# Gate weights into later tiles of the mixer, a row factor taken sooner, a cast behind the root, and turned tiles of both tokens scaled together

## The chip, the cores and the metric

The kernel runs on one core of one Trainium2 chip. The metric is the device time of one execution in microseconds (us). A core has a matrix engine (TensorE, PE in the profile, with its weight loads as PEld), a vector engine (VectorE, DVE), a scalar engine (ScalarE, ACT), GpSimd (POOL) and a sync engine (SyncE, SP) whose queue (SPq) issues nearly all loads. Each engine works through its own list of instructions in order; semaphores hold an instruction until the work it needs is done.

## The reference

One decoder block in fp32 with a sequence of 256 tokens, model width 2048 and feed-forward width 5632:

```
x = x + 0.5 * swiglu_ffn(rms_norm(x, ffn1_norm), ffn1 weights)
z = rms_norm(x, mix_norm) @ w_in            # 2048 -> 5120: lru_x, lru_gate, sc_b, sc_c, sc_x
xc = causal_depthwise_conv(lru_x, width 4) + bias
h  = rg_lru(xc, w_a, b_a, w_i, b_i, lam)    # gates: block-diagonal, 8 heads of 128x128, then a scan
y_lru = h * gelu(lru_gate)
y_sc  = sc_b * causal_depthwise_conv(sc_c * sc_x, width 3)
x = x + concat(rms_norm(y_lru), rms_norm(y_sc)) @ w_out
x = x + 0.5 * swiglu_ffn(rms_norm(x, ffn2_norm), ffn2 weights)
out = rms_norm(x, final_norm)
rms_norm(x, g) = x * rsqrt(mean(x*x) + 1e-6) * g
swiglu_ffn(x)  = (silu(x @ w_gate) * (x @ w_up)) @ w_down
```

## The kernel before

**Tiles.** The 256 tokens are two tiles of 128 (t = 0, 1). The width of 2048 is four chunks of 512. The residual stays in one tile, `xres`. Weights come from memory in units of 128x4x512 (1 MB): four blocks of 128 input rows by 512 columns.

**Products.** Each fp32 factor is split into a rounded part and a rest: for weights `hi` is a cast on ACT and `lo` is raw minus hi on DVE. Three products stand for one: hi by hi, hi by lo, lo by hi. PE first runs a unit's hi products, then its lo products. So the way of a unit is: SP issues the load into a room of the pool `raws` (three rooms), ACT casts it, DVE takes the rest, PE multiplies. `hi` and `lo` lie in the pool `splits` (two rooms; the feed-forward layers have one more). A room is free again when its last reader is done. Sums are held in eight PSUM banks.

**Feed-forward layers.** The two layers compute sums of products by a scheme that combines blocks, so that fewer products are needed, at the price of more additions on DVE. The start of the first layer is written out by hand in `begin` with the engines' order pinned there: PE begins with the first columns on the unscaled input, while ACT and DVE work out the row factor of the norm (`squares`, then `factor`: sum `tot_n`, `v_n`, root `s_n` on ACT, `y_n`, `q_n`, `r_n` on DVE). The first unit of up weights, `raw_u`, comes in two half loads; its cast `hi_u_start` is in three pieces.

**Norms.** A norm of the mixer or of the second layer (class `Norm`, names `nm` and `n2`) leaves out the row factor 1/sqrt(mean + eps) at first. It needs the residual turned, columns to partitions, and scaled by the gain, split into hi and lo (`xT`). The first three chunks are turned by `cross`: `part` copies the chunk of one token tile into one side of the tile `pair` as two halves of each number, a DMA of SP turns it into a `cross_` tile, and `join` puts the halves together in `pair`. Then ACT writes hi and DVE lo. These are tasks, one step of which is taken between two units (`onward`). The last chunk is turned on PE (`turn`, banks `pt_`). The row factor follows as `factor` and then `rows`: DVE builds two diagonal tiles, PE spreads them over the partitions in bank `pb_`, and DVE copies the bank to `bc`. Results are multiplied by `bc` when they leave PSUM.

**Mixer.** The input projection runs in ten groups of columns (`columns`, loop `order` from L1031), each of four units; unit u of group g has the names in_g_u, with the piece of the projection as g (0 lru_x, 1 lru_gate, 2 to 4 the short convolution; a piece has two halves, so names come twice). A group fills four banks, one per 128 columns. Behind the first group stand `flush`, `nm.factor`, `nm.rows` and the two loads of gate weights (`gate_weights`, L857), 512 KB each, which go through rooms of `raws` (`rawgate_a`, `rawgate_i`) and are split like other weights. Then `lru_x` takes the first group: `half_x` and `zx` (times `bc_nm`), the convolution `xc`, its split `xs`, and the gate products `pgate_a`, `pgate_i`, which stand on PE between the products of later units. The mixer has its own pools; `tmp(tag, name)` takes a tile from them. The tags "d" and "v" are used by the recurrence once its first gates are there, one tile of 128x1024 each.

**Order.** Outside `begin` a scheduler of the kernel language sets the order on each engine from the program and its dependences. Deferred small work (`defer`) is released between units by `pump` and `flush`.

Of the kernel before, what the change touches and what calls it, by code (L numbers as in the profile page):

```python
# [10 lines left out]
F32 = mybir.dt.float32  # L11
F32R = mybir.dt.float32r
U16 = mybir.dt.uint16
AF = mybir.ActivationFunctionType
ALU = mybir.AluOpType
AX = mybir.AxisListType

P = 128
D = 2048
S = 256  # L20
FF = 5632
NT = S // P
KD = D // P
KF = FF // P
CW = 512
NC_D = D // CW
UK = 4
NH = 8
# [21 lines left out]
def hybrid_block(ctx: ExitStack, tc: tile.TileContext, a: dict, out: bass.AP):  # L50
    nc = tc.nc
    Engine.pinned = False
    dve, act, pe = (Engine(tc, e) for e in (nc.vector, nc.scalar, nc.tensor))
# [6 lines left out]
    def defer(cost, fn):  # L60
        pending.append((cost, fn))

    def flush():
        while pending:
            pending.popleft()[1]()

    def pump(budget):

        owed[0] = min(owed[0], 0.0) + budget
        while pending and owed[0] > 0:  # L70
            cost, fn = pending.popleft()
            fn()
            owed[0] -= cost
# [5 lines left out]
    raws = ctx.enter_context(tc.tile_pool(name="raws", bufs=3, side="right"))  # L79
# [3 lines left out]
    def bank(name):  # L83
        return psum.tile([P, 512], F32, tag="ps", name=name)

    def f32(ap):
        return ap.bitcast(F32)
# [62 lines left out]
    def big(name):  # L150

        return bigs.tile([P, UK, 2 * S], F32R, tag="big", name=name)
# [39 lines left out]
    def unit(src, name):  # L192
        return parts_of(load(src, name), name)
# [6 lines left out]
    pair = const.tile([P, NT, CW], F32, name="pair")  # L200
    tasks, moving, sides = deque(), deque(), [0]

    def part(src, turned):

        sides[0] = 1 - sides[0]
        two = pair[:, sides[0]].bitcast(U16)
        act.copy(two.rearrange(flat, b=2), src.bitcast(U16).rearrange(mixed, b=2))
        nc.sync.dma_start(turned.rearrange("p (r c) -> p r c", c=P), two, transpose=True)
        return pair[:, sides[0]]

    def join(two, turned):
        tc.keep_in_program_order(act.copy(two.bitcast(U16).rearrange(mixed, b=2), turned.rearrange(flat, b=2)))
        return quad(two)

    def onward():

        if moving:
            two, _, fn = moving.popleft()
            fn(two)
        if tasks:  # L220
            key, begin, fn = tasks.popleft()
            moving.append((begin(), key, fn))

    def on_the_way():
        return {task[0] for task in tasks} | {entry[1] for entry in moving}
# [18 lines left out]
    class Norm:  # L244
# [28 lines left out]
        def cross(self, c, t, room):  # L273
            x = xres[:, t, c * CW : (c + 1) * CW]
            place = []

            def begin():
                place.append(room(f"cross_{self.name}_{c}_{t}").bitcast(U16))
                return part(x, place[0])

            def store(two):
                v = join(two, place[0])
                if t == 0:
                    self.xT[c] = big(f"xT_{self.name}_{c}")
                for j in range(UK):
                    g = self.gain[:, UK * c + j : UK * c + j + 1]
                    hi, lo = (self.xT[c][:, j, o + t * P : o + (t + 1) * P] for o in (0, S))
                    act.activation(hi, v[:, j], AF.Copy, scale=g)
                    dve.scalar_tensor_tensor(lo, v[:, j], g, f32(hi), op0=ALU.mult, op1=ALU.subtract)

            tasks.append(((self.name, c), begin, store))

# [36 lines left out]

    def columns(w, c0, xT, name):
        ps = [bank(f"ps_{name}_{f}") for f in range(4)]
        for u in range(KD // UK):
            blk = unit(w[u * UK * P : (u + 1) * UK * P, c0 : c0 + CW], f"{name}_{u}")
            assert ("nm", u) not in on_the_way()
            for half in range(2):
                for j in range(UK):
                    x = xT[u][:, j, :]
                    for f in range(4):  # L340
                        wf = blk[j][half][:, f * P : (f + 1) * P]
                        if half == 0:
                            pe.matmul(ps[f], wf, x, start=u == 0 and j == 0, stop=False)
                        else:
                            end = u == KD // UK - 1 and j == UK - 1
                            pe.matmul(ps[f][:, :S], wf, x[:, :S], start=False, stop=end)
            onward()
            pump(1.5)
        return ps

    def product(w, c, us, y, name):
        ps = [bank(f"ps_{name}_{t}") for t in range(NT)]
        cs = slice(c * CW, (c + 1) * CW)
        for i, u in enumerate(us):
            blk = unit(w[u * UK * P : (u + 1) * UK * P, cs], f"{name}_{u}")
            multiply([(ps[t], stationary(y(u), t), i == 0, i == len(us) - 1) for t in range(NT)], blk)
            pump(1.5)
        return ps  # L360
# [36 lines left out]
    def quad(tile):  # L397
        return tile.rearrange("p (j c) -> p j c", j=UK)
# [72 lines left out]
    def ffn(tag, norm, after, opening=False):  # L471
        with (
# [67 lines left out]
            ps = {(m, t): bank(f"ps_{m}{tag}_0_{t}") for m in "gu" for t in range(NT)}  # L540
            ws = {"g": wg, "u": wu}

            def first_columns(m, u, **how):
                return load(ws[m][u * UK * P : (u + 1) * UK * P, :CW], f"{m}{tag}_0_{u}", **how)

            def begin():
# [4 lines left out]
                raw = {("g", 0): first_columns("g", 0, pieces=pieces)}  # L551
# [58 lines left out]
                units.extend(big(f"x{tag}_{u}") for u in range(4))  # L610
                ru, (hi, lo, blk) = raw["u", 0], splits_of("u_start")
                act.copy(hi[:, :2], ru[:, :2])
                act.copy(hi[:, 2:3], ru[:, 2:3])
                norm.squares(3, (dve, act), lambda: pair[:, 0])
                norm.factor()
                act.copy(hi[:, 3:], ru[:, 3:])
                dve.tensor_tensor(lo, ru, f32(hi), op=ALU.subtract)
                n = tokens(1)
                rows = [stationary(norm.xT[0], t) for t in range(NT)]
# [231 lines left out]
    nm = held["nm"]  # L851


    with tc.tile_pool(name="mixer", bufs=1) as mp, tc.tile_pool(name="mixw", bufs=2) as mw:
        wgate = {}

        def gate_weights(key, src):  # L857
            raw = raws.tile([P, NH, P], F32, tag="raw", name=f"rawgate_{key}")
            nc.sync.dma_start(raw, src.rearrange("h i j -> i h j"))
            both = bigs.tile([P, 2, NH, P], F32R, tag="big", name=f"gate_{key}")  # L860
            hi, lo = both[:, 0], both[:, 1]
            act.copy(hi, raw)
            dve.tensor_tensor(lo, raw, f32(hi), op=ALU.subtract)
            wgate[key] = (hi, lo)
# [4 lines left out]
        w_in = a["w_in"][0]  # L869
# [3 lines left out]
        def tmp(tag, name, w=S, dt=F32, bufs=2):  # L873
            return mw.tile([P, w], dt, tag=tag, name=f"{tag}_{name}", bufs=bufs)
# [61 lines left out]
        def finish(y, k, gain, grp, first):  # L936
            sq = tmp("ysq", k)
            act.activation(sq, y, AF.Square)
            ac = acc[:, grp, :]
            if first:  # L940
                dve.tensor_copy(ac, sq)
            else:
                dve.tensor_tensor(ac, ac, sq, op=ALU.add)
            hi, lo = yT[k // UK][:, k % UK, :S], yT[k // UK][:, k % UK, S:]
            act.activation(hi, y, AF.Copy, scale=gain)
            dve.scalar_tensor_tensor(lo, y, gain, f32(hi), op0=ALU.mult, op1=ALU.subtract)
# [73 lines left out]
        def sc_b(ps, half):  # L1020
            if any(4 * half + f not in ys for f in range(4)):
                flush()
            for f in range(4):
# [4 lines left out]
                dve.tensor_tensor(y, b, y, op=ALU.mult)  # L1028
                defer(0.8, lambda q=q, y=y: finish(y, NH + q, vec["sc_out_norm"][:, q : q + 1], 1, q == 0))

        order = [  # L1031
            (lru_x, 0, 0), (lru_x, 0, 1), (sc_c, 3, 0), (lru_gate, 1, 0), (sc_x, 4, 0),
            (lru_gate, 1, 1), (sc_c, 3, 1), (sc_x, 4, 1), (sc_b, 2, 0), (sc_b, 2, 1),
        ]
        for i, (use, piece, half) in enumerate(order):
            ps = columns(w_in, piece * (D // 2) + half * CW, nm.xT, f"in_{piece}_{half}")
            if i == 0:
                flush()
                nm.factor()
                nm.rows(lambda name: tmp("half", name, bufs=4))  # L1040
                bc = nm.bc
                dve.tensor_tensor(bc2, bc, bc, op=ALU.mult)
                gate_weights("a", a["lru_w_a"][0])
                gate_weights("i", a["lru_w_i"][0])
                yT += [big(f"yT_{u}") for u in range(KD // UK)]
            use(ps, half)

# [4 lines left out]
        for c in range(NC_D):  # L1052
            cs = slice(c * CW, (c + 1) * CW)
            for g in range(2):
                if c == 0 and g == 1:
                    flush()
                ps = product(w_out, c, (2 * g, 2 * g + 1), yT.__getitem__, f"o{c}_{g}")
# [92 lines left out]
```

## Time and profile before

| | us |
|---|---|
| median of 3 runs | 1722.84 (1720.89 to 1723.07) |
| the profiled execution | 1723.02 |
| its span, first to last instruction | 1721.2 |
| PE busy | 1700.1 (99%) |
| DVE busy | 1477.9 (86%) |
| ACT busy | 1166.3 (68%) |
| memory read | 339.82 MB, 199 GB/s over the span |
| mean granted clock of PE | 0.997 |

All times of the timeline are us from the start of the span. The profile names an instruction by what it writes and reads (out<-in), with the numbers of tiles left out, so that units of one kind read alike and are told apart by their time. The granted clock (PEclk) is the share of full speed that the throttle granted to PE. A wait is named by the instruction that came last before the waiting one could go.

### The profile page before, as it was taken

Reading aid. Unit: us, or ns where it says so; the run is one execution under the profiler, and the core shown is the slowest. Engines: PE = TensorE matmul, PEld = TensorE weight load, DVE = VectorE, ACT = ScalarE, POOL = GpSimd, SP = SyncE. Lnnn points to the kernel's source line nnn. Section 1 sums busy time; section 2 is a strip of 40 time slices with the busy share of each in tenths; the row PEclk is TensorE's granted clock in tenths of the full one; section 3 lists DMA queues with packets and bytes.
Section 4 is the critical chain, followed back from the end, with each engine's and each line's share of the span. In section 5 each row is a group of like instructions: output and inputs, shape, how many; then the busy total and the mean of one; then the engine's idle time right before and its main releaser. Section 6 shows DMA issues by size and latency. Waiting matters only on the chain.

```text
span 1721.2 us, 20206 instructions
## 1 busy us (share of the span) xinstructions
PE 1700.1 (99%) x7811; PEld 1413.6 (82%) x7811; DVE 1477.9 (86%) x1286; ACT 1166.3 (68%) x1481; POOL 6.9 (0%) x32
## 2 busy tenths in 40 slices
PE   8999999999999999999999999999999999999997
PEld 6888888888887887888888888888888888887886
DVE  7988999989889878687987679989989888889796
ACT  6767667676568678765765776786667675677864
POOL 1000000000000000000000000000000000000000
PEclk9999999999999999999999999999999999999999
DMA  8667567585567685746555674585677656566853
GB/s 296 204 212 207 195 220 217 198 280 178 180 215 226 213 250 144 236 155 207 174 191 179 218 262 153 198 268 195 208 218 225 208 192 223 196 214 202 249 192 122
DMA packets 233056, 357.91 MB, mean 208 GB/s; under 512 B 64772, under 2 KB 67200, under 8 KB 232832
## 3 DMA queue, kind: packets, MB, share of 16 engines
q1 hardware_dynamic: 232496, 355.50, 63.9%
q8 instruction: 61, 1.00, 0.2%
q10 hardware_dynamic: 144, 1.05, 0.2%
q14 instruction: 35, 0.29, 0.0%
q0 software_dynamic: 320, 0.07, 0.0%
HBM read 339.82 MB, written 2.10 MB: 199 GB/s over the span
## 4 chain that ended last, share of the span: by engine, by line
PE 88%; DVE 4%; ACT 3%; DMA 2%; issue 2%; SPq 0%; DVEq 0%; ACTq 0%
PE ps_d L43 13%; PE ps_in L43 12%; PE ps_u_a L43 8%; PE ps_g_a L43 8%; PE ps_u_c L43 6%; PE ps_g_c L43 6%; PE ps_o L43 5%; PE ps_d_a L43 5%; PE ps_g_d L43 4%; PE ps_u_d L43 3%; PE ps_g_e L43 3%; PE ps_u_e L43 3%; PE ps_d_c L43 3%; PE ps_d_d L43 2%; PE ps_u L43 2%
## 5 line engine op out<-in xcount | busy, mean ns | idle before, releaser
L43 DVE TENSOR_TENSOR lo_u_p<-raw_u,hi_u_p 128x2048 fp32r<-128x2048 f32 (+1 forms) x80 | 160.0, 2019 | 18.7 <-ACT hi_u_p L43 18.2
L43 ACT CAST hi_u_p<-raw_u 128x1024 fp32r<-128x1024 f32 x140 | 141.6, 1048 | 48.9 <-PE ps_u_a L43 14.7
L43 ACT CAST hi_g_p<-raw_g 128x1024 fp32r<-128x1024 f32 x132 | 133.9, 1047 | 59.2 <-DVE raw_g L43 24.2
L43 PE MATMUL ps_d<-hi_d,h 128*128 128x512 f32 x704 | 167.0, 389 | 0.0
L43 DVE TENSOR_TENSOR lo_g_p<-raw_g,hi_g_p 128x2048 fp32r<-128x2048 f32 (+1 forms) x75 | 151.2, 2031 | 17.3 <-ACT hi_g_p L43 16.8
L43 PE MATMUL ps_in<-xT_nm,hi_in 128*128 128x512 f32 x640 | 154.5, 393 | 2.7 <-DVE bc_nm L43 2.7
L43 PEld LDWEIGHTS ps_d<-hi_d,h 128*128 128x128 f32 x704 | 132.1, 188 | 27.4
L43 PEld LDWEIGHTS ps_in<-xT_nm,hi_in 128*128 128x128 f32 x640 | 118.0, 189 | 26.3 <-DVE bc_nm L43 3.2
L43 ACT CAST hi_d_p<-raw_d 128x1024 fp32r<-128x1024 f32 x84 | 86.1, 1048 | 68.1 <-DVE raw_d L43 24.4
L43 DVE TENSOR_TENSOR lo_d<-raw_d,hi_d 128x2048 fp32r<-128x2048 f32 x44 | 100.2, 2289 | 32.9 <-ACT hi_d L43 32.7
L43 DVE TENSOR_TENSOR lo_in<-raw_in,hi_in 128x2048 fp32r<-128x2048 f32 x40 | 91.4, 2286 | 34.5 <-ACT hi_in L43 33.1
L43 ACT CAST hi_in<-raw_in 128x1024 fp32r<-128x1024 f32 x80 | 80.1, 1046 | 59.4 <-PE ps_in L43 38.8
L43 ACT CAST hi_u_x<-raw_u 128x1024 fp32r<-128x1024 f32 x80 | 81.3, 1047 | 41.8 <-PE ps_u_c L43 28.8
L43 DVE TENSOR_TENSOR lo_d_p<-raw_d,hi_d_p 128x2048 fp32r<-128x2048 f32 (+1 forms) x48 | 96.5, 2020 | 12.3 <-ACT hi_d_p L43 12.0
L43 DVE TENSOR_TENSOR raw_u<-raw_u,raw_u 128x2048 f32<-128x2048 f32 (+1 forms) x50 | 92.3, 1862 | 11.6 <-DMA raw_u<-in_ffn_w_up_dram 11.0
L43 ACT CAST hi_d<-raw_d 128x1024 fp32r<-128x1024 f32 x88 | 88.9, 1045 | 18.9 <-PE ps_d_d L43 7.6
L43 ACT CAST hi_g_x<-raw_g 128x1024 fp32r<-128x1024 f32 x80 | 81.6, 1045 | 28.3 <-PE ps_g_c L43 11.5
L43 DVE TENSOR_TENSOR lo_g_x<-raw_g,hi_g_x 128x2048 fp32r<-128x2048 f32 x40 | 91.4, 2286 | 5.6 <-ACT hi_g_x L43 5.6
L43 DVE TENSOR_TENSOR lo_u_x<-raw_u,hi_u_x 128x2048 fp32r<-128x2048 f32 x40 | 91.4, 2284 | 1.9 <-ACT hi_u_x L43 1.7
L43 DVE TENSOR_TENSOR raw_g<-raw_g,raw_g 128x2048 f32<-128x2048 f32 (+1 forms) x46 | 85.0, 1867 | 6.3 <-DMA raw_g<-in_ffn_w_gate_dram 6.2
L43 PE MATMUL ps_d<-lo_d,h 128*128 128x512 f32 x352 | 87.3, 389 | 0.0
L43 PEld LDWEIGHTS ps_in<-xT_nm,lo_in 128*128 128x128 f32 x640 | 82.5, 192 | 3.2
(399 smaller groups left out, 3671.5 us busy)
## 6 DMA issues: line engine op xcount, KB each, us to landing
raw_d<-in_ffn_w_down_dram SPq DMA_DIRECT2D x88, 1024.0 KB, 5.6
raw_u<-in_ffn_w_up_dram SPq DMA_DIRECT2D x87, 1024.0 KB, 5.3
raw_g<-in_ffn_w_gate_dram SPq DMA_DIRECT2D x86, 1024.0 KB, 5.4
raw_in<-in_w_in_dram SPq DMA_DIRECT2D x40, 1024.0 KB, 5.1
raw_o<-in_w_out_dram SPq DMA_DIRECT2D x16, 1024.0 KB, 5.1
xres<-in_x_dram SPq DMA_DIRECT2D x4, 512.0 KB, 7.5
raw_u<-in_ffn_w_up_dram SPq DMA_DIRECT2D x2, 512.0 KB, 9.2
raw_g_first<-in_ffn_w_gate_dram SPq DMA_DIRECT2D x1, 1024.0 KB, 11.9
```

The lines of the kernel that those rows point to most:

```text
L43: ins = getattr(self.engine, name)(*args, **kwargs)
```

## The change

There are four parts.

1. In `cross` the side of `pair` is fixed by the token tile (t = 0 uses side 1, t = 1 side 0). Token tile 0 only joins. When token tile 1 is joined, both are scaled together: per block of 128 columns one ACT and one DVE instruction of 128x256 in place of two each of 128x128. This holds for the three chunks of `nm` and the three of `n2`.
2. `gate_weights` takes its raw tiles from the mixer's tags "d" and "v" and no longer from `raws`.
3. `columns` calls a function behind each unit; for the first group it is `row_factor`, which runs `flush` and `nm.factor` behind unit 1 and `nm.rows` behind unit 2.
4. In `begin` the cast of the third quarter of `hi_u_start` stands behind `squares` and `factor`, with that of the last quarter.

```diff
@@ class Norm, cross
             def begin():
+                sides[0] = 1 - t
                 place.append(room(f"cross_{self.name}_{c}_{t}").bitcast(U16))
                 return part(x, place[0])
 
             def store(two):
-                v = join(two, place[0])
-                if t == 0:
-                    self.xT[c] = big(f"xT_{self.name}_{c}")
+                join(two, place[0])
+                if t < NT - 1:
+                    return
+                self.xT[c] = big(f"xT_{self.name}_{c}")
                 for j in range(UK):
                     g = self.gain[:, UK * c + j : UK * c + j + 1]
-                    hi, lo = (self.xT[c][:, j, o + t * P : o + (t + 1) * P] for o in (0, S))
-                    act.activation(hi, v[:, j], AF.Copy, scale=g)
-                    dve.scalar_tensor_tensor(lo, v[:, j], g, f32(hi), op0=ALU.mult, op1=ALU.subtract)
+                    v = pair[:, :, j * P : (j + 1) * P]
+                    hi, lo = (self.xT[c][:, j, o : o + S].rearrange("p (t c) -> p t c", t=NT) for o in (0, S))
+                    act.activation(hi, v, AF.Copy, scale=g)
+                    dve.scalar_tensor_tensor(lo, v, g, f32(hi), op0=ALU.mult, op1=ALU.subtract)
@@ columns
-    def columns(w, c0, xT, name):
+    def columns(w, c0, xT, name, between=None):
...
             pump(1.5)
+            if between:
+                between(u)
@@ begin
                 act.copy(hi[:, :2], ru[:, :2])
-                act.copy(hi[:, 2:3], ru[:, 2:3])
                 norm.squares(3, (dve, act), lambda: pair[:, 0])
                 norm.factor()
-                act.copy(hi[:, 3:], ru[:, 3:])
+                for j in (2, 3):
+                    act.copy(hi[:, j : j + 1], ru[:, j : j + 1])
@@ mixer
-        def gate_weights(key, src):
-            raw = raws.tile([P, NH, P], F32, tag="raw", name=f"rawgate_{key}")
+        def gate_weights(key, src, room):
+            raw = tmp(room, f"gate_{key}", NH * P, bufs=1).rearrange("p (h j) -> p h j", h=NH)
...
+        def row_factor(u):
+            if u == 1:
+                flush()
+                nm.factor()
+            elif u == 2:
+                nm.rows(lambda name: tmp("half", name, bufs=4))
...
-            ps = columns(w_in, piece * (D // 2) + half * CW, nm.xT, f"in_{piece}_{half}")
+            between = row_factor if i == 0 else None
+            ps = columns(w_in, piece * (D // 2) + half * CW, nm.xT, f"in_{piece}_{half}", between)
             if i == 0:
-                flush()
-                nm.factor()
-                nm.rows(lambda name: tmp("half", name, bufs=4))
                 bc = nm.bc
...
-                gate_weights("a", a["lru_w_a"][0])
-                gate_weights("i", a["lru_w_i"][0])
+                gate_weights("a", a["lru_w_a"][0], "d")
+                gate_weights("i", a["lru_w_i"][0], "v")
```

SP's queue at the step from the first to the second group of columns, before:

```order
L165 DMA raw_in_0_3_5266<-in_w_in_dram 128x4x512
L859 DMA rawgate_a<-in_lru_w_a_dram 128x8x128
L859 DMA rawgate_i<-in_lru_w_i_dram 128x8x128
L165 DMA raw_in_1_0_5371<-in_w_in_dram 128x4x512
L165 DMA raw_in_1_1_5432<-in_w_in_dram 128x4x512
```

and after:

```order
L165 DMA raw_in_0_3_5263<-in_w_in_dram 128x4x512
L165 DMA raw_in_1_0_5347<-in_w_in_dram 128x4x512
L864 DMA d_gate_a<-in_lru_w_a_dram 128x8x128
L864 DMA v_gate_i<-in_lru_w_i_dram 128x8x128
L165 DMA raw_in_1_1_5408<-in_w_in_dram 128x4x512
```

Unit 1_0 has moved ahead of both gate loads, and unit 1_1 still follows them.

DVE at the same place, from the rest of unit 0_3 to the first work on the group's results, before:

```order
L43 TENSOR_TENSOR gate_a<-rawgate_a,gate_a 128x1024
L43 TENSOR_TENSOR lo_in_0_3_5269<-raw_in_0_3_5266,hi_in_0_3_5268 128x2048
L43 TENSOR_TENSOR gate_i<-rawgate_i,gate_i 128x1024
L43 TENSOR_TENSOR lo_in_1_0_5374<-raw_in_1_0_5371,hi_in_1_0_5373 128x2048
L43 TENSOR_TENSOR lo_in_1_1_5435<-raw_in_1_1_5432,hi_in_1_1_5434 128x2048
L43 COPY bc_nm<-pb_nm 128x256
L43 TENSOR_TENSOR half_x_5343<-ps_in_0_0_5111,half_x_5343 128x256
L43 TENSOR_TENSOR bc_5110<-bc_nm 128x256
```

and after:

```order
L43 TENSOR_TENSOR gate_a<-d_gate_a,gate_a 128x1024
L43 TENSOR_TENSOR gate_i<-v_gate_i,gate_i 128x1024
L43 TENSOR_TENSOR lo_in_0_3_5266<-raw_in_0_3_5263,hi_in_0_3_5265 128x2048
L43 TENSOR_TENSOR lo_in_1_0_5350<-raw_in_1_0_5347,hi_in_1_0_5349 128x2048
L43 COPY bc_nm<-pb_nm 128x256
L43 TENSOR_TENSOR bc_5085<-bc_nm 128x256
L43 TENSOR_TENSOR lo_in_1_1_5411<-raw_in_1_1_5408,hi_in_1_1_5410 128x2048
L43 TENSOR_TENSOR half_x_5319<-ps_in_0_0_5086,half_x_5319 128x256
```

The copy `bc_nm` has moved ahead of the rest of unit 1_1, and `gate_i` ahead of the rest of unit 0_3. On PE the products `pb_nm` move in the same way, from behind the products of unit 0_3 to behind those of unit 0_2.

ACT at the start of the first feed-forward layer, before:

```order
L43 CAST hi_u_start<-raw_u_0_0_128 128x1024
L43 CAST hi_u_start<-raw_u_0_0_128 128x512
L43 ACTIVATE junk_n_3_1_206,ss_n_111<-xres 128x512
L43 ACTIVATE s_n_211<-v_n_210 128x2
L43 CAST hi_u_start<-raw_u_0_0_128 128x512
L43 ACTIVATE n_1_0_223<-xres,r_n_214 128x512
```

and after:

```order
L43 CAST hi_u_start<-raw_u_0_0_128 128x1024
L43 ACTIVATE junk_n_3_1_205,ss_n_111<-xres 128x512
L43 ACTIVATE s_n_210<-v_n_209 128x2
L43 CAST hi_u_start<-raw_u_0_0_128 128x512 x2
L43 ACTIVATE n_1_0_223<-xres,r_n_213 128x512
```

The square `junk_n` and the root `s_n` have moved ahead of the third quarter's cast; `n` follows the last quarter in both.

## The prediction

> **What bounds the kernel now.** First the page: busy time of each engine, in us and as a share of the span of 1721.2 us.
>
> ```profile
> PE 1700.1 (99%) x7811; PEld 1413.6 (82%) x7811; DVE 1477.9 (86%) x1286; ACT 1166.3 (68%) x1481; POOL 6.9 (0%) x32
> ```
>
> PE has 21 us in which it does nothing. Time saved on DVE or ACT reaches the end only where PE waits for it, so I read next what PE waited for (total, times, longest), and here its largest wait behind the first loads:
>
> ```profile
> PE ps_in L43 <- DVE bc_nm L43: 2.7, 1, 2.7
> ```
>
> It is one wait, at the step from the first to the second group of input-projection columns. Two smaller ones near the change, of 0.56 and 0.59 us, stand in rows further down. The timeline there (start, length, engine, operation, and in brackets the idle time before it with its releaser):
>
> ```profile
> 703.58 0.37 SPq L859 DMA_DIRECT2D rawgate_a<-in_lru_w_a_dram  x1
> 714.52 0.37 SPq L859 DMA_DIRECT2D rawgate_i<-in_lru_w_i_dram  x1
> 717.23 14.06 SPq L165 DMA_DIRECT2D raw_in<-in_w_in_dram  x5
> 719.85 2.46 PE L43 MATMUL ps_in<-xT_nm,hi_in 128*128 128x512 f32 x10
> 722.55 1.99 ACT L43 CAST hi_in<-raw_in 128x1024 fp32r<-128x1024 f32 x2 [2.77 <-DMA raw_in<-in_w_in_dram]
> 724.58 2.29 DVE L43 TENSOR_TENSOR lo_in<-raw_in,hi_in 128x2048 fp32r<-128x2048 f32 x1 [3.54 <-ACT hi_in L43]
> 725.42 0.60 PE L43 MATMUL pb_nm<-half_diag_nm,ones 128*128 128x128 f32 x4
> 725.78 2.78 PE L43 MATMUL ps_in<-xT_nm,hi_in 128*128 128x512 f32 x11
> 726.58 2.00 ACT L43 CAST hi_in<-raw_in 128x1024 fp32r<-128x1024 f32 x2 [2.04 <-DMA raw_in<-in_w_in_dram]
> 728.61 2.29 DVE L43 TENSOR_TENSOR lo_in<-raw_in,hi_in 128x2048 fp32r<-128x2048 f32 x1 [1.74 <-ACT hi_in L43]
> 730.82 0.42 DVE L43 COPY bc_nm<-pb_nm 128x256 f32<-128x256 f32 x1
> 731.29 2.50 PE L43 MATMUL ps_in<-xT_nm,hi_in 128*128 128x512 f32 x5 [2.73 <-DVE bc_nm L43]
> 735.74 2.46 PE L43 MATMUL ps_in<-xT_nm,hi_in 128*128 128x512 f32 x10
> ```
>
> Read it backwards. PE stops at 728.56 (725.78 + 2.78): the fourth sum of the new columns needs the bank that holds pb_nm, and that is free only when DVE has copied bc_nm at 730.82. The copy stands behind lo_in of unit 1_1 (728.61), this behind its cast (726.58), and the cast waited for its load. The loads are late because two of the three rooms of raws went to the gate weights: unit 1_0 was issued at 717.23 (first of the x5) where rawgate_a was issued at 703.58, and unit 1_1 after that.
>
> What the stop costs is more than its 2.73 us. Unit 1_0 ran on PE from 725.78 to 735.74, 9.96 us. An undisturbed unit (hi, lo, then the next work):
>
> ```profile
> 748.30 3.80 PE L43 MATMUL ps_in<-xT_nm,hi_in 128*128 128x512 f32 x16
> 751.94 2.08 PE L43 MATMUL ps_in<-xT_nm,lo_in 128*128 128x256 f32 x16
> 753.86 0.40 PE L43 MATMUL pgate_a<-xs,gate_a 128*128 128x256 f32 x2
> ```
>
> It takes 753.86 - 748.30 = 5.56 us, so the place costs 9.96 - 5.56 = 4.40 us. The rest of it is clock (stretch, length and PE busy, PEld, DVE, ACT, POOL busy, then PEclk):
>
> ```profile
> 728.50:731.20 2.70, 0.06 (x1) 0.00 (x0) 2.59 (x3) 1.17 (x5) 0.00 (x0) 0.91 0.96 349
> 731.20:733.60 2.40, 2.31 (x6) 1.83 (x7) 2.40 (x9) 0.60 (x1) 0.00 (x0) 0.50 0.62 161
> 733.60:735.70 2.10, 2.10 (x17) 2.10 (x16) 1.67 (x5) 1.83 (x3) 0.00 (x0) 0.87 0.87 339
> ```
>
> After the stop the granted clock was 0.50 for 2.40 us and 0.87 for 2.10: 0.50 x 2.40 + 0.13 x 2.10 = 1.5 us lost, and 2.73 + 1.5 = 4.2, close to the 4.40.
>
> [...]
>
> **The start.** Timeline of the first unit of the up weights, then the first PE row of the chain that ended last that is followed by PE alone:
>
> ```profile
> 12.88 1.05 ACT L43 CAST hi_u_start<-raw_u 128x1024 fp32r<-128x1024 f32 x1 [0.64 <-DMA raw_u<-in_ffn_w_up_dram]
> 14.31 0.69 DVE L43 SCALAR_TENSOR_TENSOR pair<-xres 128x512 f32<-128x512 f32 x1
> 15.59 0.62 ACT L43 CAST hi_u_start<-raw_u 128x512 fp32r<-128x512 f32 x1 [1.66 <-DMA raw_u<-in_ffn_w_up_dram]
> 16.12 0.63 ACT L43 ACTIVATE junk_n<-xres 128x512 f32<-128x512 f32 x1
> 17.27 0.20 ACT L43 ACTIVATE s_n<-v_n 128x2 f32<-128x2 f32 x1 [0.43 <-DVE v_n L43]
> 17.38 0.60 ACT L43 CAST hi_u_start<-raw_u 128x512 fp32r<-128x512 f32 x1
> 18.03 1.20 PE L43 MATMUL ps_u<-hi_u_start,xT_n 128*128 128x512 f32 x4 [0.56 <-ACT hi_u_start L43]
> 18.21 2.29 DVE L43 TENSOR_TENSOR lo_u_start<-raw_u,hi_u_start 128x2048 fp32r<-128x2048 f32 x1
> 19.54 1.03 ACT L43 CAST hi_g_next<-raw_g 128x1024 fp32r<-128x1024 f32 x1
> 20.55 2.12 PE L43 MATMUL ps_u<-lo_u_start,xT_n 128*128 128x512 f32 x8
> ```
>
> ```profile
> 35.86 5.49 PE ps_g L43 x23
> ```
>
> ACT is idle from 13.93 until the second half of raw_u lands at 15.57, and the square sum junk_n stands behind that cast, though its data are there. From there ACT and DVE carry the chain up to 35.86; PE, mostly busy, is never far from them.
>
> **The change, part by part.**
>
> *Gate rooms and row factor* go together. The gate weights now go to the tiles "d" and "v", so raws keeps its three rooms for w_in. Unit 1_0 takes SP's place and room of rawgate_a: issue about 703.58 instead of 717.23. A load takes 722.55 - 717.23 = 5.3 us from issue to cast, so it is there at about 709. Unit 1_1 takes the room for which rawgate_i was issued at 714.52 and is there at about 719.8. The gate loads are issued behind unit 1_0, once the last turned tile is joined, about 705.5, with two or three transfers under way at once; bounded by one and two such load times they land at 711 to 716.
>
> The row factor moves PE's two pb_nm products one unit sooner, from 725.42 to before unit 0_3 at 719.85, and the copy bc_nm from behind lo_in_1_1 to behind lo_in_1_0. With data there, ACT's cast of unit 1_0 follows that of unit 0_3 and waits at most until PE frees its split; lo_in_1_0 follows at about 720.1 to 722.4 and bc_nm ends at about 722.8. PE wants that bank at 726.5 (the new order takes the four banks in turn, so it is the fourth product, some 0.7 us into the unit at 725.78): slack 3.7 us, so that unit 1_0's load could be 3 us late. So the stop is gone whole: **-4.40 us**. Its lower end is the idle time alone, -2.73, if the clock falls for another reason.
>
> What does late next? DVE's chain from the end of lo_in_1_1 to the cast of the first xs, for which the gate products on PE wait:
>
> ```profile
> 736.77 0.39 ACT L43 CAST xs<-xc 128x256 fp32r<-128x256 f32 x1
> ...
> 738.04 0.28 PE L43 MATMUL pgate_a<-xs,gate_a 128*128 128x256 f32 x1
> ```
>
> Before, it took 736.77 - 730.90 = 5.87 us, with two copies of 0.42 in it that now come sooner: 5.03. After, unit 1_1 is cast when PE frees unit 0_3's split near 723.9, so lo_in_1_1 ends at about 728.25, and xs is there at 728.25 + 5.03 + 0.39 = 733.7. PE wants it at 738.04 - 4.40 = 733.6. That is a tie: 0 to 1 us of new waiting. I take 0, since the casts before it were also held by the lateness that goes, and keep 1 for the range. The gate casts now stand on ACT ahead of the cast of unit 0_3: two of about 1 us each. That cast takes 2 us and PE wants it at 719.85; with the gates landed by 716 it is ready at about 720.0 at the latest, at 717 by the sooner bound. Cost 0, cover up to 3 us.
>
> *The start.* The third quarter's cast moves behind s_n. ACT is free at 13.93, xres of that chunk is read by DVE at 14.31, so junk_n starts at about 14.3 instead of 16.12. DVE's own square ends at 15.0 and the sum follows from junk_n's end near 15.1, so s_n stands at 15.6 instead of 17.27, and before raw_u has landed. Then the two quarter casts run from 15.7 to 16.9, the second where it ended at 17.98. Third quarter: ready at 16.3 where it was at 16.2 (15.59 + 0.62), which costs PE 0.1 at most, as its one wait there is for the fourth. So lo_u_start starts at 16.9 instead of 18.21, which is 1.3 us sooner. hi_g_next is next on ACT; 19.54 less 1.3 is 18.2. Its load, issued at 6.6, is one of several in one queue and may hold it. **-1.25 us**, with 0 (a load or DVE takes it back before 35.86) and -1.4 as the ends.
>
> *The turned tiles.* Per chunk, eight ACT and eight DVE instructions of 128x128 become four and four of 128x256. ACT's prices:
>
> ```profile
> 676.28 1.28 ACT L43 ACTIVATE xT_nm<-pair,cols_many 128x128 fp32r<-128x128 f32 x4
> 676.42 2.12 PE L43 MATMUL ps_d_a<-hi_d_x,h 128*128 128x512 f32 x8 [0.59 <-ACT u_d L43]
> ...
> 712.08 1.56 ACT L43 ACTIVATE xT_nm<-pt_nm,cols_many 128x256 fp32r<-128x256 f32 x4
> ```
>
> Eight at 1.28 / 4 make 2.56, four at 1.56 / 4 make 1.56: 1.0 us of ACT per chunk, about as much of DVE, times six chunks. All lie beside PE work. PE may gain up to the 0.59 at 676.42, where fewer ACT instructions stand near u_d. Against it, all scaling of a chunk now comes in one piece after the second token, and the next chunk's copy into pair waits for DVE to read it: up to 0.5 us beside the third chunk, where PE turns the last chunk's residual right behind it. **0**, ends -0.6 and +0.5.
>
> Sum: -4.40 - 1.25 + 0 = -5.65. The profiled execution took 1723.02 (span 1721.2 and 1.8 around it), 0.2 over the median of 1722.84; so 1717.4 for it, and **1717.2 us** for the median.
>
> **The rivals.**
>
> *A wait at the gate products* takes the stop's place. For it: the tie above. Against it: the rows behind lo_in_1_1 can move up with DVE less held. At 1 us the sum is -4.65 and 1718.2; if that stop lowers the clock as the old one did (1.5 to 1.7 us), -3.0 and 1719.8.
>
> *The stop costs its idle time alone*, and the slow clock comes whatever happens there: -2.73 - 1.25 = -3.98, 1718.9. Against it: the clock is 0.91 in the stop and 0.50 only behind it. [...]
>
> *The start gives nothing*: raw_g lands after hi_g_next would want it, or DVE's later pieces are held by loads; -4.40, 1718.4.
>
> *The change doesn't do what it says*: bc_nm still stands behind lo_in_1_0, and if that unit came 4 us later than I think the stop stays. Only the start is left: 1721.6. Against it: the room is free at 703.5.
>
> *Slower*: the gate loads crowd out unit 0_3 and their casts, ahead of it on ACT, hold it. PE then stops at 719.85 for a whole column unit's start. It decides when gate_i lands later than about 716; each us beyond that is a us of PE, and beyond 2.7 us the clock costs 1.5 more. To be slower by 0.2% it must first eat 5.65 and then 3.45, so land at about 724, 18 us after issue, where 1 MB came within 5.3. At 724: 1726.
>
> **How the numbers follow.** Forecast 0.55; wait at the gate products 0.14; idle time alone 0.07; start gives nothing 0.10; stop stays 0.07; slower 0.07. About 0.2% (3.45 us) is what a measurement of this kernel can tell from no change, so faster means under 1719.4. The forecast, the start rival, the idle rival and about half of the gate wait fall there: 0.55 + 0.10 + 0.07 + 0.07 = 0.79, taken as 0.80. Within 0.2%: the other half and the stop that stays, 0.14, and slower what is left, 0.06. The range reaches from the forecast with the better ends (-0.15 at the start, -0.6 at the turned tiles, and half a us of scatter), 1715.9, up to the gate wait with a lowered clock and the +0.5 of the turned tiles, 1720.4; outside are the stop that stays and the slower case, 0.14, and little below.
>
> **What would show it.** No wait of PE for bc_nm and a granted clock of 1.00 in the second group of columns, with unit 1_0 issued at about 703 and 5.56 us long; a PE stage that starts 4.4 us sooner behind it than ahead of it. At the start s_n at 15.6, PE's lo products at 19.25, and PE's row of 35.86 near 34.6. Wrong would show as a new wait of PE for xs or hi_in between 718 and 740 (before's times), or as DVE rows before 35.86 that keep their times.

## The result, and the profile after

The changed kernel takes 1717.84 us in the median of 14 runs (1716.88 to 1721.93), the kernel before 1722.62 of 14 (1720.87 to 1723.61). The ratio is 0.9977, with a 95% interval of 0.9969 to 0.9985: 4.8 us faster by the medians. The profiled executions took 1717.43 and 1723.02 us, 5.6 us apart.

One correction first: where the part on the kernel before says that the first number in a name such as in_1_0 is the piece of the projection, it is the half. Units 0_u and 1_u of the prediction are the first two groups, as it uses them.

The page of the changed kernel: busy time, and the chain by engine.

```profile
PE 1698.2 (99%) x7811; PEld 1413.2 (82%) x7811; DVE 1474.4 (86%) x1262; ACT 1162.3 (68%) x1457; POOL 6.9 (0%) x32
...
PE 91%; DVE 3%; ACT 3%; issue 2%; DMA 1%; SPq 0%; DVEq 0%; ACTq 0%
```

PE is busy 1.9 us less with the same 7811 products; the prediction's rows put the loss by the slow clock behind the stop at 1.5 us. DVE and ACT have 24 instructions less each. PE's waits behind the first loads, all of them down to 0.2 us:

```profile
PE ps_g_c L43 <- DVE lo_g_p L43: 1.1, 4, 0.3
PE ps_u_c L43 <- DVE lo_u_p L43: 0.6, 1, 0.6
PE ps_d_a L43 <- DVE lo_d_p L43: 0.5, 1, 0.5
PE ps_d_c L43 <- ACT s_d L43: 0.3, 1, 0.3
PE pt_nm L43 <- DVE xres L43: 0.2, 1, 0.2
```

The 2.7 us for bc_nm are gone, as are the waits for u_d and for the start's cast. The wait of 0.6 us for lo_u_p, in the second feed-forward layer, is not in the trace of the kernel before. It comes and goes: a second trace of the changed kernel (all_again) lacks it, and a kernel without three of the four parts (hold8) has 0.7 us of it. The timeline at the step to the second group of columns (start, length, engine, operation):

```profile
700.47 0.37 SPq L165 DMA_DIRECT2D raw_in<-in_w_in_dram  x1
...
703.07 0.37 SPq L864 DMA_DIRECT2D d_gate_a<-in_lru_w_a_dram  x1
...
713.11 1.07 ACT L43 CAST gate_i<-v_gate_i 128x1024 fp32r<-128x1024 f32 x1
...
714.06 2.01 ACT L43 CAST hi_in<-raw_in 128x1024 fp32r<-128x1024 f32 x2
...
721.30 0.42 DVE L43 COPY bc_nm<-pb_nm 128x256 f32<-128x256 f32 x1
...
724.55 3.82 PE L43 MATMUL ps_in<-xT_nm,hi_in 128*128 128x512 f32 x16
...
728.20 2.08 PE L43 MATMUL ps_in<-xT_nm,lo_in 128*128 128x256 f32 x16
...
730.12 2.46 PE L43 MATMUL ps_in<-xT_nm,hi_in 128*128 128x512 f32 x10
...
731.84 0.80 ACT L43 CAST xs<-xc 128x256 fp32r<-128x256 f32 x2
...
732.41 0.28 PE L43 MATMUL pgate_a<-xs,gate_a 128*128 128x256 f32 x1
```

The load of unit 1_0 is issued at 700.47, ahead of the gates; bc_nm is copied at 721.30 to 721.72, 3.5 us before PE wants the bank. Unit 1_0 runs from 724.55 to 730.12, 5.57 us where it took 9.96. The granted clock (stretch, length, then busy time of PE, PEld, DVE, ACT, POOL, then PEclk) is full behind it:

```profile
728.50:731.20 2.70, 2.70 (x20) 2.53 (x20) 2.70 (x8) 2.70 (x5) 0.00 (x0) 1.00 0.88 322
731.20:733.60 2.40, 2.40 (x14) 1.93 (x13) 2.40 (x4) 1.33 (x4) 0.20 (x2) 1.00 0.15 57
```

The start, with the first long piece of PE in the chain:

```profile
15.59 0.20 ACT L43 ACTIVATE s_n<-v_n 128x2 f32<-128x2 f32 x1 [0.49 <-DVE v_n L43]
15.70 1.12 ACT L43 CAST hi_u_start<-raw_u 128x512 fp32r<-128x512 f32 x2
...
16.86 2.29 DVE L43 TENSOR_TENSOR lo_u_start<-raw_u,hi_u_start 128x2048 fp32r<-128x2048 f32 x1 [0.28 <-ACT hi_u_start L43]
...
18.37 1.05 ACT L43 CAST hi_g_next<-raw_g 128x1024 fp32r<-128x1024 f32 x1 [0.31 <-DMA raw_g<-in_ffn_w_gate_dram]
...
19.40 2.07 PE L43 MATMUL ps_u<-lo_u_start,xT_n 128*128 128x512 f32 x8
```

```profile
34.52 5.51 PE ps_g L43 x23
```

The long piece starts at 34.52 where it started at 35.86. Set side by side, PE's rows of the two traces are 1.3 us apart from there to the end of the first layer's products (707.30 against 708.62, the second unit of the first group) and 5.6 us apart from the second unit of the second group on (730.12 against 735.74): 1.3 at the start and 4.3 in the mixer. Near 1110 us the wait for lo_u_p takes 0.4 of it back, and PE's last product ends 5.2 us sooner (1706.56 against 1711.72). The whole is 5.6 us shorter all the same, because the end behind that product took 9.01 us here and 9.47 before. That end varies by itself: it is 9.0 us long with the gate rooms alone and 9.5 with rooms and start.

### The profile page after: what moved, and what is told of

It reads as the page before. It is cut to its first block, busy times and chain, and to the rows that moved or that the text cites. A ratio compares the mean times of both kernels' runs of the same rounds, so it can differ in the third digit from the quotient of the medians.

```text
span 1715.6 us, 20160 instructions
## 1 busy us (share of the span) xinstructions
PE 1698.2 (99%) x7811; PEld 1413.2 (82%) x7811; DVE 1474.4 (86%) x1262; ACT 1162.3 (68%) x1457; POOL 6.9 (0%) x32
## 4 chain that ended last, share of the span: by engine, by line
PE 91%; DVE 3%; ACT 3%; issue 2%; DMA 1%; SPq 0%; DVEq 0%; ACTq 0%
PE ps_d L43 13%; PE ps_in L43 13%; PE ps_g_a L43 9%; PE ps_u_a L43 9%; PE ps_u_c L43 6%; PE ps_g_c L43 6%; PE ps_o L43 5%; PE ps_d_a L43 5%; PE ps_g_d L43 5%; PE ps_u_d L43 3%; PE ps_d_c L43 3%; PE ps_g_e L43 3%; PE ps_u_e L43 3%; PE ps_d_d L43 2%; PE ps_u L43 2%; PE ps_g L43 2%
```

## Experiments

Each time is a median, beside the kernel before on the same chip in the same hours (its medians: 1722.45 for the four parts alone, 1722.52 for rooms_start, no_turn, all_again and hold8, 1723.01 for hold4 and hold12, 1722.61 for pin0 and pin4). Ratios are to that kernel, with a 95% interval.

| kernel | median, us | ratio |
|---|---|---|
| start's cast alone (only_start) | 1721.77 | 0.9995 [0.9987, 1.0004] |
| gate rooms alone (only_rooms) | 1718.41 | 0.9981 [0.9972, 0.9989] |
| row factor alone (only_row) | 1722.24 | 0.9999 [0.9990, 1.0008] |
| joint scaling alone (only_turn) | 1723.13 | 1.0003 [0.9995, 1.0012] |
| rooms and start (rooms_start) | 1717.89 | 0.9972 [0.9962, 0.9983] |
| all but joint scaling (no_turn) | 1717.27 | 0.9972 [0.9960, 0.9983] |
| the whole change again (all_again) | 1717.11 | 0.9970 [0.9959, 0.9982] |
| rooms, DVE copies of 1024, 2048, 3072 columns behind bc_nm (hold4, hold8, hold12) | 1718.28, 1718.74, 1718.49 | 0.9974, 0.9978, 0.9975 |
| rooms, PE's order held (pin0) | 1720.38 | 0.9988 [0.9979, 0.9997] |
| rooms, order held, a copy of 1024 columns (pin4) | 1722.70 | 1.0004 [0.9995, 1.0013] |

### The start's cast alone

```diff
-                act.copy(hi[:, 2:3], ru[:, 2:3])
                 norm.squares(3, (dve, act), lambda: pair[:, 0])
                 norm.factor()
-                act.copy(hi[:, 3:], ru[:, 3:])
+                for j in (2, 3):
+                    act.copy(hi[:, j : j + 1], ru[:, j : j + 1])
```

> Part 4 alone: the cast of the third quarter behind the root, all else as before. My theory: the root, and with it the rest of the unit, comes 1.3 us sooner, and DVE carries that through to PE's first full stretch near 36 us; -1.2 to -1.35 us, 1721.3. Rival (loads take it back): 0, 1722.6. In both the stop of 2.7 us for bc_nm stays.

The median is 0.7 us lower, the interval reaches from 2.2 lower to 0.7 higher, and 1721.77 lies between the two theories, so the times alone don't settle it. The chain of the trace does. Its first long piece of PE, of this kernel:

```profile
34.72 5.53 PE ps_g L43 x23
```

and of the kernel with gate rooms alone, which has the old start:

```profile
36.14 5.50 PE ps_g L43 x23
```

In the five traces with the new cast this piece starts at 34.52 to 34.76, in the nine with the old one at 35.86 to 36.25. The groups don't overlap, and their means, 34.65 and 36.08, are 1.4 us apart. No load takes the gain back before 36 us; the rival falls there. The stop for bc_nm stays, 2.6 us.

### The gate rooms alone

```diff
-        def gate_weights(key, src):
-            raw = raws.tile([P, NH, P], F32, tag="raw", name=f"rawgate_{key}")
+        def gate_weights(key, src, room):
+            raw = tmp(room, f"gate_{key}", NH * P, bufs=1).rearrange("p (h j) -> p h j", h=NH)
...
-                gate_weights("a", a["lru_w_a"][0])
-                gate_weights("i", a["lru_w_i"][0])
+                gate_weights("a", a["lru_w_a"][0], "d")
+                gate_weights("i", a["lru_w_i"][0], "v")
```

> Part 2 alone: gate weights in the later tiles. The copy bc_nm still stands behind the rest of unit 1_1 on DVE. My theory: the late loads are what makes the stop, so with the loads in time the rest of unit 1_1 ends near 728.25 and the copy near 728.7, where PE wants the bank at 728.6; the stop is 0.1 to 0.3 us, the clock stays at 1.00, and the time falls by 4.1 to 4.3 us, 1718.4. Rival (the row factor's place is what counts): the stop stays above 1.5 us and the gain is under 2.

1718.41, as expected. PE at unit 1_0 of this kernel:

```profile
725.77 4.06 PE L43 MATMUL ps_in<-xT_nm,hi_in 128*128 128x512 f32 x16
729.67 2.08 PE L43 MATMUL ps_in<-xT_nm,lo_in 128*128 128x256 f32 x16
731.58 2.46 PE L43 MATMUL ps_in<-xT_nm,hi_in 128*128 128x512 f32 x10
```

The unit takes 731.58 - 725.77 = 5.81 us, 0.25 over the undisturbed 5.56. So this part carries 4.15 of the 4.40 us, with bc_nm still behind the rest of unit 1_1.

### The row factor alone

```diff
+        def row_factor(u):
+            if u == 1:
+                flush()
+                nm.factor()
+            elif u == 2:
+                nm.rows(lambda name: tmp("half", name, bufs=4))
...
+            between = row_factor if i == 0 else None
+            ps = columns(w_in, piece * (D // 2) + half * CW, nm.xT, f"in_{piece}_{half}", between)
             if i == 0:
-                flush()
-                nm.factor()
-                nm.rows(lambda name: tmp("half", name, bufs=4))
```

> Part 3 alone: the row factor sooner, gate weights still through the rooms of raws. On DVE the copy bc_nm now stands even ahead of the rest of unit 1_0, so PE can't wait for the bank. Theory A: then the stop is gone, -4.3 us, 1718.3. Theory B (mine): the loads of units 1_0 and 1_1 are as late as before, the rest of unit 1_1 ends near 730.9, the first xs is there near 736.3, and PE wants it for the gate products near 733.6; a stop of about 2.7 us moves there, and the gain is within 1 us.

1722.24, 0.2 under the kernel before. The wait for bc_nm is gone from this trace, and another stands in its place:

```profile
726.10 3.82 PE L43 MATMUL ps_in<-xT_nm,hi_in 128*128 128x512 f32 x16
729.75 2.08 PE L43 MATMUL ps_in<-xT_nm,lo_in 128*128 128x256 f32 x16
731.67 2.46 PE L43 MATMUL ps_in<-xT_nm,hi_in 128*128 128x512 f32 x10
736.07 0.39 PE L43 MATMUL pgate_a<-xs,gate_a 128*128 128x256 f32 x1 [1.95 <-ACT xs L43]
```

Unit 1_0 now takes 5.57 us, and then PE stops 1.95 us at the first gate product, because the loads are as late as before and DVE reaches xs that much later. The granted clock behind this stop stays at 1.00. The wait has moved, as theory B has it, though by 0.75 us less than the 2.7 expected. The row factor alone takes away the wait that the profile names, and not what makes it.

### Joint scaling alone, and without it

The edit of the first is the change in `cross` as shown above, of the second the other three parts.

> Part 1 alone: both tokens' turned tiles scaled by one instruction. My theory: it saves about 1 us of ACT and as much of DVE per chunk, all beside PE work; 0 us, at most -0.6 from the wait for u_d and +0.5 beside the third chunk. Rival (these engines set the pace): -2 us or more.

> The whole change without part 1 (joint scaling). My theory: joint scaling is worth 0, so 1717.2 to 1717.8 like the whole change, with a short wait for u_d at 676 back. Rival (joint scaling costs, as its run alone was 0.5 us over the kernel before): 0.5 us faster than the whole change.

1723.13, and 1717.27 beside 1717.11 for the whole change on the same chip: 0.2 us apart in the second comparison, with single times that overlap. In the trace of joint scaling alone PE's rows stand 0.8 us behind those of the kernel before ahead of its first effect (at 600 us) and 0.8 behind its last in the mixer (at 736). In the middle PE's waits differ. Of the kernel without it, and of the kernel with it alone, one wait each:

```profile
PE ps_d_a L43 <- ACT u_d L43: 0.6, 1, 0.6
```

```profile
PE ps_d_a L43 <- DVE lo_d_p L43: 0.5, 1, 0.5
```

In this pair PE doesn't wait for u_d, comes to the next products sooner, and there waits 0.5 us for a rest that DVE finishes no sooner. That joint scaling is what removes the wait for u_d isn't shown, though: of eleven traces without it five have 0.6 us of this wait, three have 0.3 and three have none; the three traces with it have none, and two of them the 0.5 us for lo_d_p. The part is worth nothing measurable; no run tells 0.2 us from 0.

### Two parts, and the whole again

> Parts 2 and 4 alone, without the sooner row factor and without the joint scaling. If the two sizes of the forecast are all there is: 1722.5 - 4.1 - 1.3, 1717.1, the same as the whole change within its scatter. If the other two parts carry something of their own, it is slower than the whole change by that.

> The changed kernel once more, beside its parts: 1717.8, and 4.7 us under the kernel before; a profile in which PE has no wait over 0.6 us behind the start.

Rooms and start alone give 1717.89, the whole change 1717.11 and, in the runs of the result, 1717.84. The differences lie within the scatter of single times (1716.77 to 1718.71 for the two parts, 1715.88 to 1718.61 for the whole). Two of four parts carry the gain as far as these runs can tell; expected were 1717.1 and 1717.8, the other way round, and up to 0.8 us of the other two parts would not stand out here. The second trace of the whole change has no wait of PE over 0.4 us behind the start, as expected.

### How much a stop costs: a longer hold on the bank

Here gate rooms alone is the base, and DVE copies more columns out of the bank behind bc_nm, so that the bank comes free later while the loads are in time.

```diff
                 yT += [big(f"yT_{u}") for u in range(KD // UK)]
+                hold = yT[0].rearrange("p j (w s) -> p (j w) s", s=S)[:, :8, :]
+                dve.tensor_copy(hold, nm.pb[:, :S].rearrange("p (w s) -> p w s", w=1).broadcast_to([P, 8, S]))
```

> Part 2 alone (1718.4), with one more DVE copy behind bc_nm, of 2048 columns out of the same bank, so that PE must wait for the bank some 2.2 us again while nothing else is late. Theory A (a stop costs its length): 1720.6 and a granted clock of 1.00 behind it. Theory B (a stop of this length also takes the clock to 0.50 for some 2.5 us): 1722.1, and 0.50 in the profile. If the clock's fall depends on when the stop falls, single times spread over both.

> As the copy of 2048 columns, but of 1024: a stop of 1.2 to 1.3 us. Theory A and theory B: 1719.6, with a granted clock of 1.00 behind the stop. A clock under 1.00 would say that still shorter stops are enough.

> As the copy of 2048 columns, with a second one of 1024: a stop of about 3.7 us. Theory A: 1722.1. [...]

All three missed: 1718.74, 1718.28 and 1718.49, within 0.4 us of the base at 1718.41, and no stop. The base ran on another chip; each stands 3.8 to 4.7 us under the kernel before on its own chip, the base 4.0. DVE and PE of the kernel with 2048 columns:

```profile
728.33 2.28 DVE L43 CAST yT<-pb_nm 128x2048 fp32r<-128x2048 f32 x1
```

```profile
725.83 3.01 PE L43 MATMUL ps_in<-xT_nm,hi_in 128*128 128x512 f32 x12
728.68 1.60 PE L43 MATMUL ps_in<-xT_nm,lo_in 128*128 128x256 f32 x12
730.11 1.80 PE L43 MATMUL ps_in<-xT_nm,hi_in 128*128 128x512 f32 x7
```

The hold is there, but PE's order is another: the lo products of the three free banks come first. The scheduler, which makes the order from the program, could hide a delay that stands in the program. Why it didn't hide the late load of the kernel before isn't shown.

### A stop that the scheduler can't move

So the order of the sixteen hi products of unit 1_0 on PE was held to that of the program, in which the fourth wants the bank; once with gate rooms alone, once with the copy of 1024 columns.

```diff
                         if half == 0:
+                            Engine.pinned = name == "in_0_1" and u == 0
                             pe.matmul(ps[f], wf, x, start=u == 0 and j == 0, stop=False)
+                            Engine.pinned = False
```

> Part 2 alone (1718.4), with PE's sixteen hi products of unit 1_0 held in the order of the program, so that the fourth waits for bc_nm, from about 726.6 to 728.4: a stop of 1.9 us in place of the 0.2 that part 2 alone has. Theory A (a stop costs its length): 1720.1. Theory B (a stop long enough takes the clock to 0.50 as well): 1720.1 if 1.9 us is too short, as one execution of part 3 alone with a stop of 1.95 us and a clock of 1.00 has it; 1721.6 if not.

> The same with the added DVE copy of 1024 columns (1.22 us) out of the bank behind bc_nm, so that the stop is about 3.1 us. [...] Theory B: half clock behind the stop, 1722.8 to 1723.

Without the copy, PE and the clock behind the stop:

```profile
726.52 0.94 PE L43 MATMUL ps_in<-xT_nm,hi_in 128*128 128x512 f32 x3
729.15 3.24 PE L43 MATMUL ps_in<-xT_nm,hi_in 128*128 128x512 f32 x13 [1.70 <-DVE bc_nm L43]
...
734.15 0.86 PE L43 MATMUL ps_in<-xT_nm,hi_in 128*128 128x512 f32 x3
```

```profile
729.00:731.20 2.20, 2.04 (x9) 1.71 (x10) 2.20 (x8) 0.61 (x2) 0.00 (x0) 1.00 0.55 114
```

With the copy:

```profile
725.27 0.94 PE L43 MATMUL ps_in<-xT_nm,hi_in 128*128 128x512 f32 x3
729.12 4.81 PE L43 MATMUL ps_in<-xT_nm,hi_in 128*128 128x512 f32 x13 [2.92 <-DVE yT L43]
...
735.69 1.11 PE L43 MATMUL ps_in<-xT_nm,hi_in 128*128 128x512 f32 x4
```

```profile
729.00:731.20 2.20, 2.08 (x5) 1.74 (x6) 2.20 (x7) 0.80 (x2) 0.00 (x0) 0.54 0.89 317
731.20:733.60 2.40, 2.40 (x9) 1.87 (x9) 2.40 (x8) 0.90 (x2) 0.00 (x0) 0.71 0.33 127
```

The stop of 1.70 us leaves the clock at 1.00; the unit takes 734.15 - 726.52 = 7.63 us, 2.07 over the undisturbed 5.56. The stop of 2.92 us takes the clock to 0.54 and 0.71 in the mean of these stretches; the unit takes 10.42 us, 4.86 over. The stop is 1.22 us longer and the cost 2.8. The clock's loss is 0.46 x 2.2 + 0.29 x 2.4 = 1.7 us, and with the 1.22 us of length that makes 2.9, close to the 2.8. The medians point the same way: 1720.38 and 1722.70, 2.3 us apart.

In this pair of traces theory B holds, with the late loads out of the way.

In the traces the length of PE's idle time is not all that counts, though. Cut finely, the clock of the kernel before, at the stop and behind PE's last product, which ends at 1711.72:

```profile
730.70:730.80 0.10, 0.00 (x0) 0.00 (x0) 0.10 (x1) 0.00 (x0) 0.00 (x0) 0.60 1.10 430
730.80:734.10 3.30, 2.81 (x8) 2.33 (x9) 3.30 (x11) 0.83 (x2) 0.00 (x0) 0.50 0.74 231
734.10:734.20 0.10, 0.10 (x3) 0.10 (x3) 0.10 (x1) 0.10 (x1) 0.00 (x0) 0.83 0.89 348
...
1713.70:1713.80 0.10, 0.00 (x0) 0.00 (x0) 0.09 (x2) 0.00 (x0) 0.00 (x0) 0.80 0.00 0
```

Worked out from the shares in these short stretches, it falls to 0.50 at 730.72, while PE still stands and 2.16 us after it stopped, comes back at 734.13, 3.41 us later, and falls again at 1713.76, 2.04 us behind PE's last product. Worked out in the same way from its two rows above, the half clock at the stop of 2.92 us runs from 729.18, 0.1 us after PE has gone on, to 732.59, 3.41 us as well.

In the kernel with the order held and no copy PE ends at 1710.01, and the clock is still at 1.00 in a stretch of 3.40 us in which PE does nothing:

```profile
1711.80:1715.20 3.40, 0.00 (x0) 0.00 (x0) 1.88 (x6) 1.15 (x3) 0.00 (x0) 1.00 0.35 124
1715.20:1715.30 0.10, 0.00 (x0) 0.00 (x0) 0.00 (x0) 0.00 (x0) 0.00 (x0) 0.59 1.00 369
```

Here the fall comes at 1715.22, 5.21 us behind PE's last product, where it took 2.04 us in the kernel before. What sets its moment isn't shown, and with one trace of each of these kernels neither is whether a stop of 2.7 or 2.9 us takes the clock down in every execution. Whether that is what spreads the single times with the stop of 2.92 us (1721.19 to 1726.17, against 1719.13 to 1720.86 with that of 1.70) stays open: the traced execution, with its fall, is at 1721.91 one of the three shortest of eleven. Its mean clock over the span, 0.998, doesn't tell either, for a half clock behind PE's last product, as the trace of the kernel before has it, counts in such a mean too.

## Why the prediction was right, by its own steps

The forecast was 1717.2 with a range of 1715.9 to 1720.4; 1717.84 and, in a second set, 1717.11 were measured. For the profiled execution it was 1717.4, and 1717.43 was measured.

- **Gate rooms and row factor, -4.40.** The traces give 9.96 - 5.57 = 4.39 us at unit 1_0, and 4.3 between the rows ahead of it and behind. The mechanism held: loads in time, no stop, full clock. Unit 1_0 was issued at 700.47, some 3 us sooner than the 703 named, which only adds slack. What the prediction did not do is part the two edits, which it took together. Rooms alone give 4.15 of it by the trace, the row factor adds 0.25 at most, and by itself it only moves the wait to the gate products.
- **The cost of a stop, 4.40 and not 2.73.** Right for the profiled execution, and the held order shows the cause apart from the loads. The prediction read 0.50 only behind the stop, where the fine cut has the fall 0.6 us before its end, and took the loss of clock as part of the stop in every execution, which one trace of the kernel before can't show.
- **The tie at the gate products.** It came out on the good side: the casts of the first two xs run from 731.84 to 732.64, so the first is done about 732.2; the product ran at 732.41, and the trace lists no wait there. The prediction's 733.7, less the 1.3 us of the start, is 732.4. The margin is 0.2 us, which the prediction could not have told from a short wait; taking 0 there was in part luck. The row factor alone shows what was at stake, 1.95 us.
- **Gate casts ahead of unit 0_3 on ACT.** Hidden, as costed: gate_i was cast at 713.11 and unit 0_3 at 714.06, and no load is named in front of either.
- **The start, -1.25.** The root was predicted at 15.6 and stood at 15.59, the rest of the unit at 16.9 (16.86), PE's lo products at 19.25 (19.40), the piece at 34.6 (34.52). The size was a little low: 1.4 us over fourteen traces. hi_g_next was held by its load, by 0.31 us, as the prediction feared; the piece behind it came no later than forecast.
- **The turned tiles, 0.** In the profiled execution the wait for u_d was gone and a wait of 0.5 us stood in its place, with 0.2 us for pt_nm beside the third chunk. The first can come without the change, as shown above; no time tells the part from 0.
- **What the sum left out.** That 1717.43 came within 0.1 us of 1717.4 is in part luck: the two sizes hold (5.6 us at 735), but 0.4 us went to the wait for lo_u_p and 0.5 came back in the end behind PE's last product, and the prediction weighed neither. The sum was made on the trace before and compared with medians. The medians moved by 4.8 us in the first set and 5.4 in the second, against 5.65. Single times of the kernel before spread over 2.7 us, and some of the changed kernel were at 1720 to 1722. What made those late isn't known; no trace caught one.

## What to carry to other kernels

When PE waits for a small instruction, look at what stands ahead of that instruction on its engine and what that waits for: here a row factor was named, and loads made late by two rooms of a load buffer, lent to other weights, were the cause. Moving the named instruction alone moved the wait one step down; giving the loads their rooms back took away nearly all of it. Cost a stop by the whole unit against an undisturbed one, since the clock behind the stop can cost more than half as much again (4.40 us for a stop of 2.73).

## What the runs showed of the hardware

Stops of PE of 1.70 and 1.95 us, one trace each, left the granted clock at 1.00. At stops of 2.73 and 2.92 us, one trace each, it went to 0.50 for 3.41 us; the fall came 2.16 us into the first, and 0.1 us after PE had gone on behind the second. Behind PE's last product it fell after 2.04 us in the kernel before and after 5.21 us in the kernel with the order held and no copy. How long a stop must be for a fall wasn't measured.
